# Attention's sums over keys: one 512-column matmul for the high and low parts of the weights in place of two of 256

## The chip, the cores and the metric

The kernel runs on one core of a Trainium2 chip. The metric is the device time of one execution in microseconds; the time before is the median of three runs. The profile is of one more execution, taken by the hardware profiler.

## What is computed

One decoder layer on 2048 tokens of width 1024, float32. Two groups of eight heads (64 wide) attend causally: a stick-breaking group (reference, cut) and a forgetting group; each group's output is normed per head and goes through one output projection, and a gated MLP with a short convolution follows.

```
# stick-breaking, z = q k / 8, strictly causal
log_a = log_sigmoid(z) + (sum over later keys of log_sigmoid(-z))
a     = where(strict, exp(log_a), 0);   out = a @ v
# forgetting, F = cumsum(log f)
p     = softmax(where(causal, q k / 8 + F[t] - F[s], -inf));   out = p @ v
```

The change is in the step `a @ v` or `p @ v`, the sum over keys.

## The kernel before

Each float32 operand of a matmul is split in two: a high part that the matmul's rounded format (fp32r) holds, and a low part, the difference. A product is then summed from high times high, high times low and low times high. `split` (lines 43 to 45) makes the parts: ACT writes the high one, DVE or POOL subtracts it from the source.

Stages, by time in the trace: from 0 to some 90 us the conditioning, the first norm and projection; to some 925 us the stick-breaking group; to some 1610 us the forgetting group; then the output projection, the MLP's up-projection (from 1800 us) and the down-projection (from 2670 us to the end). While attention runs, the projections of later heads (lines 268 and 310) are put between its steps on PE, a few at a time, by `fill_proj`.

Attention works by **units** (a pair of heads and 512 queries; 32 of them), in each four **heads** (`Head`: one head and 256 queries, `j2` and `hl`), in each head some **items** that make the weights for up to 512 keys, and for each pair of key tiles a **group** (`Group`: 2 tiles of 128 keys by 2 tiles of 128 queries). There are 128 heads and 576 groups. 128 of the groups lie on the diagonal (`diag`, one for each head): there the later keys with the earlier queries give nothing, and that quarter is zero.

A stick-breaking item: two matmuls make the logits (lines 368, 369), ACT takes two sigmoids (457, 458), DVE runs a product scan along the keys (463, 466, 470), and POOL multiplies (471), which gives the weights `a`, queries on partitions. A forgetting item: DVE adds the decay and takes the running minimum (510), ACT the exponential (515).

A group then has two steps. `turn` (line 377): PE transposes its four 128 by 128 blocks into one PSUM bank `ps_pt` (383; three where the group is diagonal); on the diagonal POOL writes zeros into the missing quarter of both parts of `at` (386); ACT copies the bank to the high part (387); DVE subtracts to get the low part (388). `at` has three buffers and holds `[2 parts, 4 blocks of 128]` with the blocks in the order (second key tile, query 0), (first, 0), (first, 1), (second, 1). `add` (line 390): four matmuls into the head's PSUM bank `ps_pv`, which has one buffer: for each of the two key tiles, the high and then the low part, 256 queries wide. The stationary operand is V of that key tile and head, 64 columns of its high part beside 64 of its low part, so rows 0 to 63 of the result are V's high part and rows 64 to 127 its low part; all four matmuls add to the same 256 columns. A group's `add` is called two groups after its `turn`.

```
for w in range(2):
    rhs = at[:, w].rearrange("p (s q) -> p s q", q=P)[:, 0:4:3, :] if kk else at[:, w, P:3 * P]
    nc.tensor.matmul(o[:, 0:2 * P], head.V[kt // 4][:, kt % 4, head.hl, :], rhs, ...)
```

`finish` (line 418) ends a head: ACT copies rows 64 to 127 to `o2` (421), DVE adds them to rows 0 to 63 into `oT` (422). After the second of two heads POOL squares `oT` (556, `sq`), PE sums the squares some groups later (561), and after the fourth an SP DMA stores `oT` (426).

The program's order on each engine is set when it is built: the tile framework schedules by an own model of the time, from the order of the code. Each engine runs its queue in order, and waits are on semaphores that the framework places.

Of the kernel before, what the change touches and what calls it, by code (L numbers as in the profile page):

```python
# [8 lines left out]
F32 = mybir.dt.float32  # L9
F32R = mybir.dt.float32r  # L10
BF16 = mybir.dt.bfloat16
AF = mybir.ActivationFunctionType
# [4 lines left out]
P = 128  # L17
# [3 lines left out]
HD = 64  # L21
# [12 lines left out]
def kernel(ctx: ExitStack, tc: tile.TileContext, x, c, w_ada, b_ada, g_attn, w_in, b_fgate,  # L34
                      g_out_fox, g_out_sb, w_out, g_mlp, w_up, conv_w, conv_b, w_down, g_final, out):
    nc = tc.nc
# [3 lines left out]
    def f(t):  # L40
        return t.bitcast(F32)
# [91 lines left out]
    def open_pool(name, side=None, space=None):  # L133
        st = pools[name] = ExitStack()
        kw = dict(space=space) if space is not None else {}
        return st.enter_context(tc.tile_pool(name=name, bufs=1, side=side, reuse_waits="tile", **kw))
# [8 lines left out]
    sb = open_pool("sb", side="right")  # L145
# [226 lines left out]
    class Group:  # L372
# [5 lines left out]
        def turn(self):  # L378
            b = pt()
            self.at = at = sb.tile([P, 2, 2 * 2 * P], F32R, name="at", bufs=3)  # L380
            for i, (kk, qi) in enumerate([(1, 0), (0, 0), (0, 1), (1, 1)]):
                if not (self.diag and i == 0):
                    nc.tensor.transpose(b[:, i * P:(i + 1) * P], self.blk(self.kts[kk], qi), ident)  # L383
            lo = P if self.diag else 0
            if self.diag:
                nc.gpsimd.memset(f(at[:, :, 0:P]), 0.0)
            nc.scalar.activation(at[:, 0, lo:], b[:, lo:], AF.Copy)  # L387
            nc.vector.tensor_sub(at[:, 1, lo:], b[:, lo:], f(at[:, 0, lo:]))  # L388

        def add(self):  # L390
            head, at = self.head, self.at
            if self.first:
                head.o = pv()
            o = head.o
            for kk, kt in enumerate(self.kts):
                for w in range(2):
                    rhs = at[:, w].rearrange("p (s q) -> p s q", q=P)[:, 0:4:3, :] if kk else at[:, w, P:3 * P]
                    nc.tensor.matmul(o[:, 0:2 * P], head.V[kt // 4][:, kt % 4, head.hl, :], rhs,  # L398
                                     start=self.first and kk == 0 and w == 0, stop=self.last and kk == 1 and w == 1)
            if self.last:  # L400
                head.finish()

    class Head:
# [13 lines left out]

        def finish(self):
            o, oT, hl, j2 = self.o, self.unit.oT, self.hl, self.j2
            o2 = sb.tile([HD, 2 * P], F32, name="o2", bufs=2)  # L420
            nc.scalar.activation(o2, o[HD:P, 0:2 * P], AF.Copy)
            nc.vector.tensor_add(oT[hl * HD:(hl + 1) * HD, j2 * 2 * P:(j2 + 1) * 2 * P], o[0:HD, 0:2 * P], o2)
            if hl:
                self.unit.head_var(j2)
                if j2:
                    nc.sync.dma_start(os_[self.unit.mp][self.unit.tb], oT)
# [48 lines left out]
    class FoxItem:  # L475
# [11 lines left out]
        def weights(self, qi, ch):  # L487
            head, n = self.head, self.head.n
            W = (2 * head.j + qi + 1) * P
            Fb = Fbs[head.unit.p][head.hl]  # L490
            ls = head.unit.ls
            if ch == 0:
                self.mn = None
                if n > 2:
                    self.rows[qi] = sx.tile([P, S], F32, name="p", bufs=4)
                elif qi == 0:
                    both = sx.tile([P, S], F32, name="p", bufs=4)
                    self.rows = [both[:, 0:S // 2], both[:, S // 2:S]]
            a = self.rows[qi]
            need = min(512, W - ch * 512)  # L500
            b = logits(max(need, 2 * P), head.qcols(qi), head.hl, head.Q, head.K[ch])
            cuts = [(0, need, Fb[ch][:, :need])]
            if ch == n - 1:
                diag = sx.tile([P, P], F32, name="Fd", bufs=3)
                nc.gpsimd.affine_select(out=diag, in_=Fb[ch][:, need - P:need], pattern=[[-1, P]],
                                        base=0, channel_multiplier=1, compare_op=ALU.is_ge, fill=BIG)
                cuts = [(0, need - P, Fb[ch][:, :need - P])] * (need > P) + [(need - P, need, diag)]
            for lo, hi, add in cuts:
                m2 = sx.tile([P, 1], F32, name="mn", bufs=8)
                nc.vector.tensor_tensor_reduce(out=a[:, ch * 512 + lo:ch * 512 + hi], in0=b[:, lo:hi], in1=add,  # L510
                                               scale=1.0, scalar=3e38 if self.mn is None else self.mn, op0=ALU.add,
                                               op1=ALU.min, accum_out=m2)
                self.mn = m2
            if ch == n - 1:
                nc.scalar.activation(a[:, 0:W], a[:, 0:W], AF.Exp, scale=-1.0, bias=self.mn,
                                     accum_out=ls[:, head.hl, head.qc + qi:head.qc + qi + 1])
# [569 lines left out]
    def load(k, tb):  # L1086
        n = P if k < NFULL else REST
        g = dp.tile([P, 2, TB], F32R, name="g", bufs=6)
        wraw = dp.tile([P, D], F32, name="wdraw", bufs=3)
        graw = dp.tile([P, TB], F32, name="graw", bufs=2)  # L1090
        w = dp.tile([P, 2, D], F32R, name="wd", bufs=6)
        for r in range(P // n):
            nc.sync.dma_start(wraw[r * n:(r + 1) * n], w_down[k * P:k * P + n, :])
            nc.sync.dma_start(graw[r * n:(r + 1) * n], gs[k][tb // 2][:, tb % 2 * TB:(tb % 2 + 1) * TB])
        split(w[:, 0], w[:, 1], wraw, nc.vector)
        if n == P:
            split(g[:, 0], g[:, 1], graw)
        else:
            nc.scalar.activation(g[:, 0], graw, AF.Copy)
            nc.vector.tensor_sub(g[REST:P, 0], graw[REST:P], f(g[REST:P, 0]))  # L1100
        return g, w
# [6 lines left out]
    for tb in range(NTB):  # L1108
# [13 lines left out]
        for k in range(NKD):  # L1122
            g, w = load(k, tb)
# [55 lines left out]
```

## Time and profile before

| | |
|---|---|
| median of 3 runs | 3153.06 us (3152.79 to 3157.4) |
| span of the profiled execution | 3151.1 us |
| PE busy in it | 2971.6 us, 94% |
| PE weight loads | 2517.7 us, 80% |
| DVE, ACT, POOL busy | 68%, 53%, 41% |
| the sums over keys (line 398) | 2304 matmuls, 437.8 us busy |
| granted TensorE clock | 0.98 of full speed over the span |

A matmul's busy time includes the modelled drain of its pipeline; what it keeps from the next matmul is the distance from start to start, which is read from merged rows of the timeline. Idle time stands with the instruction that it precedes, and names what ended it. The chain of waits is followed back from the last instruction.

### The profile page before, as it was taken

What the parts mean: (1) busy time and instruction counts of PE and PEld (TensorE: products, weight loads), DVE (VectorE), ACT (ScalarE), POOL (GpSimd) and SP (SyncE); (2) the same over time, 40 slices, a digit from 0 to 9 for tenths busy, and PEclk for the clock granted to TensorE, in tenths of its full rate; (3) what the DMA queues carried; (4) which work ended last, traced back from release to release, by engine and by line L of the source; (5) the groups of instructions that cost most, each with busy time, mean ns of one, the idle gap of its engine ahead of it and who ended that gap; (6) DMA issues with size and microseconds to landing.
All of it is one profiled execution on the core that took longest, in us unless ns stands there. A gap on an engine that the chain in (4) does not pass through costs nothing.

```text
span 3151.1 us, 46387 instructions
## 1 busy us (share of the span) xinstructions
PE 2971.6 (94%) x15934; PEld 2517.7 (80%) x15934; DVE 2138.4 (68%) x3422; ACT 1655.3 (53%) x3033; POOL 1306.8 (41%) x1459
## 2 busy tenths in 40 slices
PE   7889898989989999999999999999899998999998
PEld 5778797878878889887877778888678887888887
DVE  6776689787976776556743577777987776254253
ACT  5565577666765565556743444444544444343332
POOL 2673566666653242242212244444444442332321
PEclk8999999999999999999999999999999999999999
DMA  9439633654236685685546632222222223554552
GB/s 266 169 133 300 193 106 97 215 180 134 76 115 213 219 288 180 185 301 169 170 153 219 213 96 85 83 88 85 84 81 82 87 86 123 190 201 158 192 200 90
DMA packets 292939, 496.51 MB, mean 158 GB/s; under 512 B 29448, under 2 KB 177664, under 8 KB 291680
## 3 DMA queue, kind: packets, MB, share of 16 engines
q1 hardware_dynamic: 281072, 480.92, 47.9%
q10 hardware_dynamic: 11632, 12.63, 1.1%
q8 instruction: 126, 2.06, 0.3%
q14 instruction: 109, 0.89, 0.1%
HBM read 352.61 MB, written 90.51 MB: 141 GB/s over the span
## 4 chain that ended last, share of the span: by engine, by line
PE 51%; DVE 14%; DMA 13%; POOL 9%; issue 7%; ACT 4%; SPq 2%; POOLq 0%; DVEq 0%; ACTq 0%
PE ps_pj L268 8%; PE ps_o L1118 8%; PE ps_pv L398 6%; PE ps_pt L383 5%; PE ps_pj L310 5%; PE ps_o L968 4%; PE ps_t L1118 4%; PE ps_bc L1118 4%; DMA wuraw<-in_w_up_dram 3%; PE ps_qk L368 3%; DVE wu L45 3%; PE ps_qk L369 3%; DMA hp<-hs 2%; DVE u L1037 2%; POOL ws L956 2%
## 5 line engine op out<-in xcount | busy, mean ns | idle before, releaser
L968 PE MATMUL ps_o<-oa,wu 128*128 128x512 f32 x2088 | 502.7, 392 | 12.6 <-DVE oa L45 5.8
L968 PEld LDWEIGHTS ps_o<-oa,wu 128*128 128x128 f32 x2088 | 391.1, 188 | 102.5 <-DVE oa L45 9.6
L398 PE MATMUL ps_pv<-at,V 128*128 128x256 f32 x2304 | 437.8, 300 | 21.3 <-DVE at L388 8.8
L388 DVE TENSOR_TENSOR at<-ps_pt,at 128x512 fp32r<-128x512 f32 (+1 forms) x576 | 365.1, 650 | 122.4 <-ACT at L387 119.6
L268 PE MATMUL ps_pj<-hp,w_qk 128*128 128x512 f32 x1512 | 417.2, 407 | 17.7 <-DMA hp<-hs 5.5
L387 ACT ACTIVATE at<-ps_pt 128x512 fp32r<-128x512 f32 (+1 forms) x576 | 319.1, 576 | 193.0 <-PE ps_pt L383 132.5
L471 POOL TENSOR_TENSOR a<-a,rw 128x512 f32<-128x512 f32 (+2 forms) x272 | 317.2, 1176 | 234.8 <-DVE rw L466 68.3
L398 PEld LDWEIGHTS ps_pv<-at,V 128*128 128x128 f32 x2304 | 341.8, 192 | 57.9 <-DVE at L388 18.5
L268 PEld LDWEIGHTS ps_pj<-hp,w_qk 128*128 128x128 f32 x1512 | 276.2, 192 | 73.6 <-DMA hp<-hs 7.2
L45 DVE TENSOR_TENSOR wd<-wdraw,wd 128x1024 fp32r<-128x1024 f32 x88 | 112.7, 1280 | 261.9 <-ACT wd L44 261.8
L45 POOL TENSOR_TENSOR g<-graw,g 128x512 fp32r<-128x512 f32 x84 | 142.7, 1702 | 325.8 <-ACT g L44 325.8
L368 PE MATMUL ps_qk<-K,Q 128*128 128x512 f32 (+2 forms) x640 | 260.7, 408 | 14.9 <-ACT a L458 7.1
L466 DVE TENSOR_TENSOR_SCAN rw<-rw 128x512 f32<-128x512 f32 x168 | 251.4, 1509 | 18.0 <-ACT rw L457 16.9
L1118 PE MATMUL ps_o<-wd,g 128*128 128x512 f32 x1040 | 251.1, 391 | 8.7 <-ACT g L44 8.7
L968 PE MATMUL ps_t<-ob,wu 128*128 128x512 f32 x984 | 244.0, 393 | 0.0
L310 PE MATMUL ps_pj<-w_v,hp 128*128 128x256 f32 (+1 forms) x1536 | 230.8, 293 | 9.8 <-DVE V L45 4.6
L369 PE MATMUL ps_qk<-K,Q 128*128 128x512 f32 (+2 forms) x640 | 236.7, 371 | 0.0
L1118 PEld LDWEIGHTS ps_o<-wd,g 128*128 128x128 f32 x1040 | 196.2, 189 | 49.9 <-ACT g L44 9.1
L44 ACT ACTIVATE wu<-wuraw 128x512 fp32r<-128x512 f32 x214 | 133.2, 626 | 195.8 <-PE ps_o L968 132.4
L383 PE MATMUL ps_pt<-edge,a 128*128 128x128 f32 x1088 | 189.8, 280 | 43.0 <-POOL a L471 37.5
L310 PEld LDWEIGHTS ps_pj<-w_v,hp 128*128 128x128 f32 x1536 | 209.8, 195 | 17.3 <-issue 8.7
L968 PEld LDWEIGHTS ps_t<-ob,wu 128*128 128x128 f32 x984 | 187.0, 190 | 39.4 <-ACT hf_m L873 0.2
(222 smaller groups left out, 5753.7 us busy)
## 6 DMA issues: line engine op xcount, KB each, us to landing
hp<-hs SPq DMA_DIRECT2D x224, 512.0 KB
wuraw<-in_w_up_dram SPq DMA_DIRECT2D x84, 512.0 KB
wdraw<-in_w_down_dram SPq DMA_DIRECT2D x84, 512.0 KB
Q<-q SPq DMA_DIRECT2D x128, 256.0 KB
g<-u SPq DMA_DIRECT2D x42, 512.0 KB
graw<-g SPq DMA_DIRECT2D x84, 256.0 KB
hs<-hp SPq DMA_DIRECT2D x32, 512.0 KB
K<-q SPq DMA_DIRECT2D x128, 128.0 KB
```

What stands on the lines that cost most here:

```text
L45: (lo_engine or nc.gpsimd).tensor_sub(lo, src, f(hi))
L268: nc.tensor.matmul(acc, w[kt][:, a, n], h[:, bb], start=kt == 0 and i == 0, stop=kt == KT - 1 and i == 2)
L310: nc.tensor.matmul(av[:, t * width:(t + 1) * width], hts[kt][:, a, tok], w[1][kt][:, bb, 0:width], start=kt == 0 and m == 0, stop=kt == KT ...
L368: nc.tensor.matmul(b[:, :cw], Q[:, hl, 0, qcols], K[:, hl, :cw], start=True, stop=False)
L369: nc.tensor.matmul(b[:, :cw], Q[:, hl, 1, qcols], K[:, hl, :cw], start=False, stop=True)
L383: nc.tensor.transpose(b[:, i * P:(i + 1) * P], self.blk(self.kts[kk], qi), ident)
L387: nc.scalar.activation(at[:, 0, lo:], b[:, lo:], AF.Copy)
L388: nc.vector.tensor_sub(at[:, 1, lo:], b[:, lo:], f(at[:, 0, lo:]))
L398: nc.tensor.matmul(o[:, 0:2 * P], head.V[kt // 4][:, kt % 4, head.hl, :], rhs, start=self.first and kk == 0 and w == 0, stop=self.last and ...
L471: nc.gpsimd.tensor_mul(a[:, :need], a[:, :need], r[:, 1:need + 1])
L968: nc.tensor.matmul(b, w[:, p, j], o[:, q], start=first and i == 0, stop=last and i == 2, skip_group_check=True)
L1118: nc.tensor.matmul(banks[t][n], g[:, a, t * P:(t + 1) * P], w[:, b, n * TB:(n + 1) * TB], start=k == 0 and i == 0, stop=k == NKD - 1 and i ...
```

## The change

On PE, `add` takes two matmuls for a group instead of four. The moving operand is both parts of two blocks, 512 columns; the high part's sums go to columns 0 to 255 of the bank, the low part's to columns 256 to 511. On the diagonal the second key tile's matmul covers only the later query tile, 2 times 128 columns, so nothing reads the empty quarter and POOL no longer writes zeros. `finish` has three sums to add instead of two: ACT copies two pieces out of PSUM, DVE adds the third from PSUM, and POOL adds the last two into `oT`. V's low part times the weights' low part, which was in the sum before, is left out. `o2` has the same room, but one buffer of all 128 partitions instead of two of 64.

```diff
             lo = P if self.diag else 0
-            if self.diag:
-                nc.gpsimd.memset(f(at[:, :, 0:P]), 0.0)
             nc.scalar.activation(at[:, 0, lo:], b[:, lo:], AF.Copy)
             nc.vector.tensor_sub(at[:, 1, lo:], b[:, lo:], f(at[:, 0, lo:]))
...
             for kk, kt in enumerate(self.kts):
-                for w in range(2):
-                    rhs = at[:, w].rearrange("p (s q) -> p s q", q=P)[:, 0:4:3, :] if kk else at[:, w, P:3 * P]
-                    nc.tensor.matmul(o[:, 0:2 * P], head.V[kt // 4][:, kt % 4, head.hl, :], rhs,
-                                     start=self.first and kk == 0 and w == 0, stop=self.last and kk == 1 and w == 1)
+                if not kk:
+                    out_, rhs = o, at[:, :, P:3 * P]
+                elif self.diag:
+                    out_, rhs = o.rearrange("p (w q) -> p w q", w=2)[:, :, P:2 * P], at[:, :, 3 * P:4 * P]
+                else:
+                    out_, rhs = o, at.rearrange("p w (s q) -> p w s q", q=P)[:, :, 0:4:3, :]
+                nc.tensor.matmul(out_, head.V[kt // 4][:, kt % 4, head.hl, :], rhs,
+                                 start=self.first and kk == 0, stop=self.last and kk == 1)
...
-            o2 = sb.tile([HD, 2 * P], F32, name="o2", bufs=2)
-            nc.scalar.activation(o2, o[HD:P, 0:2 * P], AF.Copy)
-            nc.vector.tensor_add(oT[hl * HD:(hl + 1) * HD, j2 * 2 * P:(j2 + 1) * 2 * P], o[0:HD, 0:2 * P], o2)
+            o2 = sb.tile([P, 2, 2 * P], F32, name="o2", bufs=1)[hl * HD:(hl + 1) * HD]
+            nc.scalar.activation(o2[:, 0], o[HD:P, 0:2 * P], AF.Copy)
+            nc.scalar.activation(o2[:, 1], o[0:HD, 2 * P:4 * P], AF.Copy)
+            nc.vector.tensor_add(o2[:, 0], o[0:HD, 0:2 * P], o2[:, 0])
+            nc.gpsimd.tensor_add(oT[hl * HD:(hl + 1) * HD, j2 * 2 * P:(j2 + 1) * 2 * P], o2[:, 0], o2[:, 1])
```

Lines from the loop on move by 2, those behind `finish` by 4: the sums are line 400 now, the copies 423 and 424, DVE's add 425, POOL's 426, the square 560.

What stands in the queues, on PE in a late unit of the forgetting group, around the end of a pair of heads, before:

```order
L268 MATMUL ps_pj<-hp,w_qk 128x512 x11
L398 MATMUL ps_pv<-at,V 128x256
L268 MATMUL ps_pj<-hp,w_qk 128x512
L368 MATMUL ps_qk<-K,Q 128x512
L369 MATMUL ps_qk<-K,Q 128x512
L268 MATMUL ps_pj<-hp,w_qk 128x512
L398 MATMUL ps_pv<-at,V 128x256 x3
L383 MATMUL ps_pt<-edge,p 128x128 x4
L398 MATMUL ps_pv<-at,V 128x256 x4
```

and with the change:

```order
L268 MATMUL ps_pj<-hp,w_qk 128x512 x2
L368 MATMUL ps_qk<-K,Q 128x512
L369 MATMUL ps_qk<-K,Q 128x512
L400 MATMUL ps_pv<-at,V 128x512 x2
L383 MATMUL ps_pt<-edge,p 128x128 x4
L400 MATMUL ps_pv<-at,V 128x512 x2
```

A group's first matmul stood apart from the other three, ahead of filler; now both stand together, behind the filler. Across attention the filler between the sums is dealt out anew in the same way, here as there.

On POOL at the end of the stick-breaking group, in the heads with the most keys, before:

```order
L471 TENSOR_TENSOR a<-a,rw 128x512 [waits DVE_49,PE_49,Activation_49] x2
L386 MEMSET at 128x2x128 [waits DVE_49,PE_49]
L471 TENSOR_TENSOR a<-a,rw 128x512 [waits DVE_49,Activation_49] x2
L556 TENSOR_TENSOR sq<-oT 128x256 [waits DVE_49]
L471 TENSOR_TENSOR a<-a,rw 128x512 [waits DVE_49,Activation_49] x2
```

and at the end of that group's last heads with the change:

```order
L426 TENSOR_TENSOR oT<-o_9990 64x256 [waits DVE_49,Pool_49]
L560 TENSOR_TENSOR sq<-oT 128x256 [waits Pool_49]
L509 AFFINE_SELECT Fd<-Fb 128x128 [waits DMAHW2_49]
```

The zeroing, which waited for PE to be done with the buffer, is gone; the head's add stands in POOL's queue ahead of the square and waits for DVE (`AFFINE_SELECT`, line 505 before and 509 now, masks the decay for the first forgetting heads).

On ACT, at the end of a forgetting head, before:

```order
L387 ACTIVATE at<-ps_pt 128x384
L421 ACTIVATE o_15689<-ps_pv 64x256
L387 ACTIVATE at<-ps_pt 128x512
L515 ACTIVATE p,ls<-p,mn 128x768
L387 ACTIVATE at<-ps_pt 128x512
```

and with the change:

```order
L385 ACTIVATE at<-ps_pt 128x384
L423 ACTIVATE o_14913<-ps_pv 64x256
L424 ACTIVATE o_14913<-ps_pv 64x256
L385 ACTIVATE at<-ps_pt 128x512
L44 ACTIVATE V<-ps_pj 128x4x64
```

The second copy stands right behind the first, and the framework signals both with one step of the semaphore behind the second, so DVE's add waits for both.

## Rows read from the trace of the kernel before

**Rows 1.** The page: busy time, share of the span and instructions of each engine.

```profile
PE 2971.6 (94%) x15934; PEld 2517.7 (80%) x15934; DVE 2138.4 (68%) x3422; ACT 1655.3 (53%) x3033; POOL 1306.8 (41%) x1459
```

**Rows 2.** Stretches of 100 us: length, busy us and count of each engine, clock, DMA.

```profile
core 0: us, PE busy (x) PEld busy (x) DVE busy (x) ACT busy (x) POOL busy (x), PEclk, DMA share, GB/s
500.00:600.00 100.00, 87.09 (x587) 76.41 (x586) 88.08 (x114) 72.55 (x161) 71.25 (x91) 1.00 0.38 111
800.00:900.00 100.00, 84.01 (x573) 72.94 (x572) 97.50 (x110) 77.46 (x159) 70.00 (x76) 0.97 0.16 49
1300.00:1400.00 100.00, 99.51 (x648) 89.24 (x647) 58.23 (x165) 55.16 (x101) 35.04 (x49) 1.00 0.75 249
1500.00:1600.00 100.00, 96.45 (x629) 82.97 (x628) 80.19 (x230) 67.34 (x111) 17.97 (x39) 1.00 0.46 150
2000.00:2100.00 100.00, 99.80 (x439) 81.87 (x438) 76.54 (x90) 44.81 (x65) 41.93 (x41) 1.00 0.26 79
```

**Rows 3.** The chain of waits through attention, 90 to 1610 us, by line.

```profile
by line: PE ps_pj L268 17.3%; PE ps_pv L398 12.4%; PE ps_pt L383 10.2%; PE ps_pj L310 9.2%; PE ps_qk L368 5.5%; issue 5.3%; PE ps_qk L369 5.1%; DMA hp<-hs 4.6%; DVE rw L466 3.2%; POOL a L471 2.9%; DVE at L388 2.3%; DMA hp<-in_w_ada_dram 2.1
```

**Rows 4.** PE's waits in that stretch: us in total, times, longest us.

```profile
PE ps_pt L383 <- POOL a L471: 37.5, 35, 3.0
PE ps_pv L398 <- DVE at L388: 8.8, 19, 1.2
...
PE ps_pv L398 <- ACT at L387: 6.8, 7, 1.7
...
PE ps_pv L398 <- DVE oT L422: 4.6, 7, 1.1
```

**Rows 5.** PE's timeline near 1325 us: start, us from first start to last end.

```profile
1323.02 1.11 PE L398 MATMUL ps_pv<-at,V 128*128 128x256 f32 x8
1323.98 0.38 PE L383 MATMUL ps_pt<-edge,p 128*128 128x128 f32 x2
1324.11 0.72 PE L398 MATMUL ps_pv<-at,V 128*128 128x256 f32 x4
...
1326.05 0.39 PE L268 MATMUL ps_pj<-hp,w_qk 128*128 128x512 f32 x1
...
1326.74 3.12 PE L268 MATMUL ps_pj<-hp,w_qk 128*128 128x512 f32 x13
```

**Rows 6.** Line 398 alone: count, ns min/median/max; waits of both PE rows.

```profile
L398 PE MATMUL ps_pv<-at,V x2304: 274/282/682, 80.8 to 1611.6; 128*128 128x256 f32 x192
...
  DVE at L388: 27.3, 56
  ACT at L387: 21.7, 28
  DVE oT L422: 10.3, 13
```

**Rows 7.** Groups by line: busy us, mean ns, idle us before and what ended it.

```profile
L398 PE MATMUL ps_pv<-at,V 128*128 128x256 f32 x2304 | 437.8, 300 | 21.3 <-DVE at L388 8.8 <-ACT at L387 7.4 <-DVE oT L422 4.6
...
L421 ACT ACTIVATE o<-ps_pv 64x256 f32<-64x256 f32 x128 | 48.9, 382 | 47.2 <-PE ps_pv L398 44.6
...
L422 DVE TENSOR_TENSOR oT<-ps_pv,o 64x256 f32<-64x256 f32 x128 | 52.7, 412 | 24.8 <-ACT o L421 22.9
...
L386 POOL MEMSET at<- 128x256 f32 x128 | 39.8, 312 | 172.9 <-PE ps_pv L398 150.4 <-PE ps_pt L383 9.8 <-DVE V L45 6.4
...
L556 POOL TENSOR_TENSOR sq<-oT 128x256 f32<-128x256 f32 x64 | 50.9, 795 | 67.2 <-DVE oT L422 65.1 <-PE ps_pj L310 1.0 <-PE ps_pt L561 0.8
```

**Rows 8.** POOL's multiply and square by line: count, ns min/median/max.

```profile
L471 POOL TENSOR_TENSOR a<-a,rw x272: 405/1092/2318, 268.7 to 906.4; 128x512 f32<-128x512 f32 x84, 128x128 f32<-128x128 f32 x26, 128x384 f32<-128x384 f32 x26
...
L556 POOL TENSOR_TENSOR sq<-oT x64: 609/615/1632, 93.5 to 1612.8; 128x256 f32<-128x256 f32 x64
```

**Rows 9.** POOL's timeline in a late stick-breaking unit.

```profile
514.15 2.97 POOL L471 TENSOR_TENSOR a<-a,rw 128x512 f32<-128x512 f32 x2 [0.97 <-DVE rw L466]
517.08 1.52 POOL L556 TENSOR_TENSOR sq<-oT 128x256 f32<-128x256 f32 x1
518.57 3.05 POOL L471 TENSOR_TENSOR a<-a,rw 128x512 f32<-128x512 f32 x2
```

## The prediction

> **What bounds the kernel now.** I read the page's busy shares first: PE is busy 94% of the span, DVE 68%, POOL 41% [rows 1]. An average says little here, so next come stretches of 100 us. In the forgetting half of attention PE is at 99.5 and 96.5 of 100 us, DVE at 58 and 80; in the late stick-breaking units DVE is at 88 and 97.5 while PE is at 87 and 84, and POOL at 70; in the MLP PE is full, and nothing of the change is there [rows 2]. So there are two kinds of stretch in attention: one where PE sets the pace and one where DVE and POOL do. The chain of waits from 90 to 1610 us says how they mix: the six PE lines that it lists come to 17.3 + 12.4 + 10.2 + 9.2 + 5.5 + 5.1 = 59.7% of the 1520 us, the line of the change alone to 12.4% or 188 us; DVE's scan, POOL's multiply and the `at` subtraction come to 8.4% [rows 3]. PE's largest wait is for POOL's multiply, 37.5 us [rows 4].
>
> **PE, full pairs.** A busy PE is not a full PE, so a matmul's price is its distance from start to start. Eight sums in a row take 1.11 us, the last with its own length of 0.28: (1.11 - 0.28) / 7 = 0.119 us for 256 columns [rows 5, 6]. Thirteen matmuls of 512 columns take 3.12 us, the last 0.39: 2.73 / 12 = 0.2275 us [rows 5]. So two of 256 cost 0.238, one of 512 costs 0.2275, and 0.0105 us is saved: halving the count hardly helps, since the columns streamed are the same. Of 576 groups with two key tiles each, 1152 pairs, 128 are the diagonal's second tile; the other 1024 save 10.8 us.
>
> A rule speaks against even that. The Trainium skill, "TensorE: Matmul & The Clock Gate", section "Back-to-back issue gap", puts the distance at the columns over 2.4 GHz and some 2.5 ns more, by which a pair would save only that one 2.5 ns. By an estimate from it the full pairs would give 2.6 us; the rows here have about 12 ns beside the columns at both sizes, and the measurement decides.
>
> **PE, the diagonal.** There the second tile's two matmuls of 256 columns become one of 256 (2 times 128): 128 x 0.119 = 15.2 us. Together 26.0 us of streaming, which is the safe part.
>
> **PE, waits inside a group.** The four sums at 1324.11 take 0.72 us, (0.72 - 0.28) = 0.44 for three steps instead of 0.36: 0.08 us is lost within the group, and the eight at 1323.02 lose nothing [rows 5]. The high-part matmul waits for ACT, the low-part one for DVE; a load of V that stands behind a wait isn't hidden. With one wait and one load fewer in a group this can shrink: by nothing at least, by 576 x 0.08 = 46 us at most. I take a quarter of the groups, 12 us, nearer to the row without loss. The price: the first sum can no longer start on the high part alone, so a wait for DVE (27.3 us in 56 times for both PE rows, [rows 6]) now stands ahead of both sums; since it was waited out within the group before, I put no more on it. So PE gets 38 us back (26 to 72).
>
> **How much of it reaches the end.** By the share of the chain on PE, 0.6: 23 us. From below, by the share of the line's own busy time that is on the chain, 188 of 437.8 us or 0.43 [rows 3, 7], 11 us of the streaming; from above all 72.
>
> **The longer end of a head.** ACT copies a second piece, 0.382 us [rows 7], and DVE's add (0.412 us as before) waits for both. `ps_pv` has one buffer, so the next head's first sum is released 0.382 us later, and on PE everything behind it stands in line. Sums waited for DVE's `oT` 13 times in both PE rows [rows 6], of 128 heads: 13 x 0.382 = 5 us. From below nothing, since the framework deals the filler anew; from above 127 x 0.382 = 48.5 us, if every next sum stood ready. I take 5, as the rows show few waits there. ACT itself does 128 x 0.382 = 49 us more, at 53% of the span busy and 72 to 77 in the busiest stretches [rows 1, 2]. No ACT line is among the first of the chain [rows 3], so between 0 and 49 I take 2.
>
> **POOL.** The zeroing goes: 128 x 0.312 = 39.8 us of work, and 172.9 us of standing in front of it, 150.4 of it until PE was done with `at` [rows 7]. In comes an add of 64 x 256 for each head. The nearest row is the square of 128 x 256: 0.615 us in the middle, 1.632 at most [rows 8], so 128 adds are 79 to 209 us, 39 to 169 more than the zeroing. Each waits for DVE, as the square did (65.1 us before 64 squares, [rows 7]), and behind it in POOL's queue stand the multiplies of the next heads, for which PE waits. So one head-of-line wait replaces another, and I count only the work: in the stick-breaking half 64 heads x (0.615 - 0.312) = 19 us, of which POOL's share where PE waits for it, about a sixth: 3 us. From above 64 x 1.32 = 84 us, from below minus 10 us, since the wait before the zeroing goes. `o2` has one buffer: the next head's first copy waits for this add, and a whole head's work lies between the two, so I cost it at nothing; if POOL is late by more than that, ACT stands still, and with it every `at`. On SP the store of `oT` now waits for POOL instead of DVE, some 0.6 us later, with loads of `hp` behind it; 32 stores, 19 us at most, nothing as long as loads run ahead: nothing.
>
> **Sum.** 23 - 5 - 2 - 3 = 13 us less. Profiled span 3151.1 us, median 3153.06, so 2 us or 0.06% lie around the span; the median becomes 3153.06 - 13 = **3140 us**.
>
> **Rivals.** (a) All of PE's time comes back, with half of the waits inside the groups: 26 + 23 = 49 us, 3104 us. For it: PE above 96% in the forgetting half; against it: DVE at 97.5 of 100 us late in the stick-breaking half [rows 2], where PE's gain is only idle time. (b) PE's gain is hidden: PE waits out what it saved for DVE's scan and POOL's multiply, and costs eat the rest: 3153 us, within 6. It is the case if the filler of projections is used up sooner and the stick-breaking units then run at DVE's pace; for it the 59.7% that leave 40% of the chain elsewhere [rows 3]. (c) Slower, by POOL in the stick-breaking half. The square took 1.52 us between two pairs of multiplies that followed without a gap [rows 9]; an add of that length instead of a zeroing of 0.31 is 1.2 us later for the multiplies behind it. If each of the 35 times that PE waits for a multiply [rows 4] grows by 1.2 us, that is 42 us, against 23 gained and 7 of other costs: 26 us slower, 3179 us. It decides from 16 us on, 0.46 us for each of those waits.
>
> On the length of that add: the multiplies take 1.09 us in the middle and up to 2.3 [rows 8], two lengths for one kind of work. The Trainium skill, "SBUF — State Buffer", section "SBUF: two separate sides", has DVE instructions with two inputs in SBUF and POOL's reads take the same pair of ports in turn, the whole instruction long; by it the add is long where DVE is busiest, which is where (c) needs it. The spread of the multiplies agrees; who held the port no row here shows.
>
> (d) The order. Filler, sums and transposes stand otherwise in every queue, as in the piece of PE's queue shown with the change; that is worth some 15 us either way, an estimate of one PE wait of the size seen (37.5 us in 35 times, about 1 us each, [rows 4]) for about each second of the 32 units.
>
> **Chances.** The sum as forecast, from 3128 to 3147: 0.40; (a) and what lies between it and the forecast: 0.20; (b): 0.20; (c), or (d) to that side: 0.20. A measurement of this kernel can tell some 0.2%, 6 us, from no change. So faster 0.60, same 0.20, slower 0.20. The range of 8 in 10 reaches to (a) halfway and to the middle of (c): 3110 to 3166.
>
> **What would show it.** After: 1152 sums with 0.23 us between starts, weight loads halved, PE's busy time down by about 26 us plus drains; 128 more ACT copies of 0.38 us; no zeroing on POOL. If PE's idle time grows by as much as its streaming falls, (b) holds. If the new add takes over 1 us in the stick-breaking half and PE's wait for the multiply grows beyond 37.5 us, (c) holds. If sums wait for DVE's add in far more than 13 heads, the head's end was underpriced. If starts of 512-column sums lie further apart than 0.2275 us, for instance because the moving operand is now four strips of 128 columns, 10 ns more would take 10 us from the gain and 20 ns all of the full pairs'.

## The result and the profile after

The changed kernel takes **3184.16 us** in the median, the kernel before 3154.23 in the runs beside it: ratio **1.0093, interval 1.0081 to 1.0104**, some 29 us slower where 13 us less were forecast, and above the top of the range (3166). The profiled execution of after took 3191.87 us with a span of 3190.0; the last sum of attention ends at 1645 us instead of 1612, and the up-projection starts at 1837.5 instead of 1798.9, as much later as the span is longer: the loss is made ahead of the MLP, most of it in attention. Within attention most of it falls in the stick-breaking group: ACT's first copy at the end of the 64th head, the last of that group, comes at 945.7 us instead of 918.7, and that of the 128th at 1645.7 instead of 1611.9, so 27 of 34 us are lost by then.

The page's busy times, to be read beside [rows 1]:

```profile
PE 2975.5 (93%) x14782; PEld 2446.4 (77%) x14782; DVE 2157.1 (68%) x3422; ACT 1694.2 (53%) x3161; POOL 1376.1 (43%) x1459
```

The edit is all there: 1152 matmuls fewer on PE, 128 copies more on ACT, POOL with as many instructions as before (an add for each zeroing) and 69 us more work. Yet PE's busy time hasn't fallen (the last section, on the granted clock, has part of the reason). Stretches of after, the last line the sums over five stretches from 90 to 1650 us; columns as in [rows 2]:

```profile
90.00:400.00 310.00, 270.56 (x1465) 224.69 (x1464) 209.04 (x273) 179.32 (x389) 180.97 (x213) 0.92 0.59 189
800.00:900.00 100.00, 88.96 (x497) 72.60 (x496) 94.85 (x108) 73.18 (x156) 68.23 (x74) 0.93 0.25 81
1300.00:1400.00 100.00, 96.41 (x588) 83.67 (x586) 57.44 (x173) 55.72 (x116) 35.68 (x54) 0.98 0.58 182
1500.00:1600.00 100.00, 93.11 (x529) 74.93 (x528) 81.22 (x250) 75.03 (x141) 27.56 (x53) 0.98 0.50 153
...
sum 1560.00, PE 1423.66 PEld 1179.72 DVE 1150.14 ACT 1006.51 POOL 799.92; mean PE 284.73 PEld 235.94 DVE 230.03 ACT 201.30 POOL 159.98
```

The forgetting half, where PE was full (99.5 and 96.5 in [rows 2]), has pauses now: 96.4 and 93.1. In the same 1560 us of before the sum was:

```profile
sum 1560.00, PE 1453.62 PEld 1277.13 DVE 1137.26 ACT 981.07 POOL 730.87; mean PE 290.72 PEld 255.43 DVE 227.45 ACT 196.21 POOL 146.17
```

PE is busy 30 us less in this stretch: the streaming that the edit takes away, and some of the work behind attention that now falls outside. PE got time back and spent it waiting. For what, line 400 alone shows (count, ns min/median/max; then waits of both PE rows, us and times), beside [rows 6]:

```profile
L400 PE MATMUL ps_pv<-at,V x1152: 274/396/799, 84.1 to 1645.3; 128*128 128x512 f32 x192
...
  DVE at L386: 68.4, 78
  DVE o L425: 8.4, 13
```

Waits for ACT's high part (21.7 us) are gone, those for DVE's low part went from 27.3 to 68.4 us. The waits for the head's add are as before, 13 times. The groups by line (busy us, mean ns | idle us before and what ended it), beside [rows 7]:

```profile
L386 DVE TENSOR_TENSOR at<-ps_pt,at 128x512 fp32r<-128x512 f32 (+1 forms) x576 | 364.1, 649 | 112.3 <-ACT at L385 109.5
...
L475 POOL TENSOR_TENSOR a<-a,rw 128x512 f32<-128x512 f32 (+2 forms) x272 | 313.1, 1161 | 197.5 <-DVE rw L470 51.0 <-DVE rw L467 39.5 <-PE ps_pt L383 29.6
...
L426 POOL TENSOR_TENSOR oT<-o 64x256 f32<-64x256 f32 x128 | 124.0, 969 | 189.9 <-DVE o L425 174.6 <-DVE var L571 6.8 <-PE ps_qk L369 3.3
...
L425 DVE TENSOR_TENSOR o<-ps_pv,o 64x256 f32<-64x256 f32 x128 | 52.9, 414 | 37.4 <-ACT o L424 22.1 <-PE ps_pj L268 5.6 <-PE ps_qk L369 2.0
...
L560 POOL TENSOR_TENSOR sq<-oT 128x256 f32<-128x256 f32 x64 | 49.6, 776 | 5.0 <-PE ps_pt L565 2.1
```

POOL's new add stands 189.9 us idle, nearly all for DVE. But the zeroing and the square stood 172.9 + 67.2 us idle before [rows 7]: POOL waits less than it did. The sums of waits alone don't say where 29 us went, so the parts were run one by one.

### The profile page after: what moved, and what is told of

Its sections match the earlier page's. It is cut to its first block, busy times and chain, and to the rows that moved or that the text cites. A ratio compares the mean times of both kernels' runs of the same rounds, so it can differ in the third digit from the quotient of the medians.

```text
span 3190.0 us, 44409 instructions
## 1 busy us (share of the span) xinstructions
PE 2975.5 (93%) x14782; PEld 2446.4 (77%) x14782; DVE 2157.1 (68%) x3422; ACT 1694.2 (53%) x3161; POOL 1376.1 (43%) x1459
## 4 chain that ended last, share of the span: by engine, by line
PE 42%; DVE 13%; DMA 10%; issue 7%; POOL 7%; ACT 3%; SPq 1%; POOLq 0%; ACTq 0%; DVEq 0%
PE ps_o L1122 7%; PE ps_pj L268 6%; PE ps_pv L400 4%; PE ps_t L1122 4%; PE ps_bc L1122 4%; PE ps_pt L383 4%; DMA wuraw<-in_w_up_dram 3%; PE ps_o L972 3%; DVE wu L45 3%; PE ps_pj L310 2%; PE ps_qk L368 2%; PE ps_qk L369 2%; DVE u L1041 2%; DMA hp<-hs 2%; POOL ws L960 2%
## 5 line engine op out<-in xcount | busy, mean ns | idle before, releaser
L400 PE MATMUL ps_pv<-at,V 128*128 128x512 f32 (+1 forms) x1152 | 373.4, 415 | 29.8 <-DVE at L386 26.0
L368 PE MATMUL ps_qk<-K,Q 128*128 128x512 f32 (+2 forms) x640 | 265.1, 415 | 18.9 <-DVE mn L514 11.4
L470 DVE TENSOR_TENSOR_SCAN rw<-rw 128x512 f32<-128x512 f32 x168 | 258.6, 1551 | 23.1 <-ACT rw L461 21.8
L400 PEld LDWEIGHTS ps_pv<-at,V 128*128 128x128 f32 x1152 | 196.0, 195 | 68.6 <-DVE at L386 42.4
L369 PE MATMUL ps_qk<-K,Q 128*128 128x512 f32 (+2 forms) x640 | 240.0, 376 | 0.0
L383 PE MATMUL ps_pt<-edge,a 128*128 128x128 f32 x1088 | 192.4, 285 | 47.0 <-POOL a L475 36.1
L383 PEld LDWEIGHTS ps_pt<-edge,a 128*128 128x128 f32 x1088 | 140.8, 147 | 102.0 <-POOL a L475 55.3
```

Of the source, the lines that this page charges most:

```text
L368: nc.tensor.matmul(b[:, :cw], Q[:, hl, 0, qcols], K[:, hl, :cw], start=True, stop=False)
L369: nc.tensor.matmul(b[:, :cw], Q[:, hl, 1, qcols], K[:, hl, :cw], start=False, stop=True)
L400: nc.tensor.matmul(out_, head.V[kt // 4][:, kt % 4, head.hl, :], rhs, start=self.first and kk == 0, stop=self.last and kk == 1)
```

## The experiments

Differences in us are the ratio's, times 3154; the interval of a ratio stands beside it.

**Which part: the head's end or the sums.** The head's end alone, on the kernel before (ACT copies some values a second time with a scale of 0, POOL adds these zeros):

```diff
+ o2 = sb.tile([P, 2, 2 * P], F32, name="o2", bufs=1)[hl * HD:(hl + 1) * HD]
  nc.scalar.activation(o2[:, 0], o[HD:P, 0:2 * P], AF.Copy)
+ nc.scalar.activation(o2[:, 1], o[0:HD, 0:2 * P], AF.Copy, scale=0.0)
+ nc.vector.tensor_add(o2[:, 0], o[0:HD, 0:2 * P], o2[:, 0])
+ nc.gpsimd.tensor_add(oT[...], o2[:, 0], o2[:, 1])
```

> The kernel before with the change's end of a head alone: its four sums of 256 columns and its zeroing stay; ACT makes a second copy (of sums already there, scaled by zero, so that nothing is added), DVE adds, POOL adds into oT, o2 has one buffer. Theory 1, the longer end of a head is the cause (POOL's add in front of the multiplies, a PSUM bank released later): slower than before by 20 us or more, 3174 to 3200. Theory 2, the merged sums are the cause (both now wait for the low part): 3154 to 3164. Theory 3, any edit deals the queues out anew and that alone moves the time: anywhere from 3140 to 3175, with no growth of the waits for DVE's add or POOL's multiply.

Measured (e1) 3187.24 us, 1.0102 (1.0080 to 1.0124): +32 us, the whole loss. In its profile 31 us are lost by the end of the 64th head (949.9 us) and 32 by that of the 128th (1643.7): all of it in the stick-breaking group.

The sums alone: the changed sums with the head's end of before, so the low parts of the weights are summed but left out of the result.

```diff
- nc.scalar.activation(o2[:, 1], o[0:HD, 2 * P:4 * P], AF.Copy)
- nc.vector.tensor_add(o2[:, 0], o[0:HD, 0:2 * P], o2[:, 0])
- nc.gpsimd.tensor_add(oT[...], o2[:, 0], o2[:, 1])
+ nc.vector.tensor_add(oT[...], o[0:HD, 0:2 * P], o2)
```

> The changed kernel with the end of a head as before (one copy, one add on DVE, no add on POOL, two buffers of o2): the sums of the low part of the weights, columns 256 to 511, are computed and left out of the result. Theory 1 (the end of a head): the gain of the sums is seen, 3130 to 3145. Theory 2 (the merged sums' wait): still slower than before, 3165 to 3185, and PE's waits of sums for DVE stay near 68 us in both PE rows. Theory 3: 3140 to 3175.

Measured (e2) 3152.37 us, 0.9995 (0.9984 to 1.0006): nothing. So there are two questions: why the end costs 32 us, and why 1152 matmuls fewer bring none.

**The end, piece by piece.** Only the second copy, unread, so that ACT works 49 us more and the bank is released 0.38 us later:

```diff
+ nc.scalar.activation(o2[:, 1], o[0:HD, 0:2 * P], AF.Copy)
```

> The kernel before with ACT's second copy alone at the end of a head (the same 64 by 256 piece once more, into a buffer that nobody reads; o2 has one buffer); DVE adds into oT as before, POOL is untouched. The end of a head as a whole cost 32 us. Theory 1a, the copy is the cause (0.38 us more on ACT, and the PSUM bank released 0.38 us later): 3170 to 3187. Theory 1b, POOL's add is the cause: 3150 to 3162.

Measured (e5) 3158.01 us, 1.0004 (0.9994 to 1.0015): ACT's work and the later release cost 0 to 5 us. Only POOL's add, of zeros, with DVE's add writing to `o2`:

```diff
+ nc.vector.tensor_add(o2, o[0:HD, 0:2 * P], o2)
+ nc.gpsimd.tensor_add(oT[...], o2, edge[...])
```

> The kernel before with POOL's add alone: ACT copies once, DVE adds into o2, and POOL adds zeros to that, into oT; the PSUM bank is released as early as before, o2 has two buffers. Theory 1b (oT later, and POOL's queue held by an add that waits for DVE): 3170 to 3187. Theory 1a: 3150 to 3162. If both cost half: 3165 to 3172 for each of the two.

Measured (e6) 3191.30 us, 1.0117 (1.0102 to 1.0132): +37 us. The add is the price. Two runs put it on DVE instead, once from `o2` and once straight from PSUM with one copy less:

```diff
- nc.gpsimd.tensor_add(oT[...], o2[:, 0], o2[:, 1])
+ nc.vector.tensor_add(oT[...], o2[:, 0], o2[:, 1])
```

> The changed kernel with the last add of a head on DVE in place of POOL. If POOL's add is the cause within theory 1: back to 3150 to 3165, and POOL's 175 us of standing before the add are gone. If it is the later release of the PSUM bank or the merged sums: 3175 to 3195, DVE having 0.4 us more for each of 128 heads.

```diff
- nc.scalar.activation(o2[:, 1], o[0:HD, 2 * P:4 * P], AF.Copy)
- nc.gpsimd.tensor_add(oT[...], o2[:, 0], o2[:, 1])
+ nc.vector.tensor_add(oT[...], o[0:HD, 2 * P:4 * P], oT[...])
```

> The changed kernel with one ACT copy and two adds on DVE, the second adding the low part's sums from PSUM into oT: no second copy on ACT and no POOL, but the bank is released 0.41 us later than before, as late as in the changed kernel. If the later release of the bank is the cause: 3170 to 3185, as the changed kernel with its last add on DVE (3176.7). If ACT's extra copy in its queue is the cause: 3150 to 3160.

Measured (e3) 3176.67 us, 1.0072 (1.0051 to 1.0093), and (e7) 3181.80 us, 1.0084 (1.0069 to 1.0099): +23 and +26 us. Elsewhere, then, but not gone. Both lie in the ranges expected for the later release of the bank, but e5 has that at 0 to 5 us, so the numbers alone don't name it.

**Why the add on POOL costs: its work, or what it waits for.** On the kernel before, one POOL add more in each head, into the unread half of `o2`: once of constants, once of `oT` (which DVE wrote as early as before) and constants.

```diff
+ nc.gpsimd.tensor_add(o2_unread_half, zero, zero)      # e9
+ nc.gpsimd.tensor_add(o2_unread_half, oT[...], zero)   # e10
```

> The kernel before, with one more POOL add of 64x256 in each of the 128 heads, zeros plus zeros into the unread half of o2: the work of the new add (0.73 us in the middle in the profile of after, 94 us in all) without any wait for DVE. If POOL's time itself is the price of the add, because the multiplies behind it come that much later: most of the 36 us that POOL's add cost in e6_pool_add_alone, 3180 to 3190. If the price is the waiting in POOL's queue for DVE's add, or the later oT: within 10 us of before, 3150 to 3165.

> The kernel before, DVE writes oT as it did, and one more POOL add in each head reads oT and writes the unread half of o2: the work of the new add and its wait for DVE, but oT is complete as early as before. If work is the price: as e9_pool_work. If the wait at the head of POOL's queue is: 3180 to 3190 here and near before in e9_pool_work. If it is the later oT (square and store wait for it): near before in both, 3150 to 3165.

Measured (e9) 3154.44 us, 1.0001 (0.9989 to 1.0013), and (e10) 3176.03 us, 1.0067 (1.0042 to 1.0091). Groups of POOL, of the first and then of the second:

```profile
L426 POOL TENSOR_TENSOR o<-edge 64x256 f32<-64x256 f32 x128 | 96.2, 752 | 15.9 <-DVE oT L425 5.7
...
L560 POOL TENSOR_TENSOR sq<-oT 128x256 f32<-128x256 f32 x64 | 53.3, 832 | 56.4 <-DVE oT L425 52.6 <-DMA wos<-hp 2.4 <-ACT hp L660 0.3
```

```profile
L426 POOL TENSOR_TENSOR o<-oT,edge 64x256 f32<-64x256 f32 x128 | 115.5, 902 | 144.8 <-DVE oT L425 128.5 <-DVE var L571 3.5 <-ACT w_v L44 3.4
...
L560 POOL TENSOR_TENSOR sq<-oT 128x256 f32<-128x256 f32 x64 | 50.5, 789 | 7.4 <-PE ps_pt L565 2.5
```

96 us of work that waits for nothing cost nothing; 115 us of work that waits for DVE cost 21 us. The wait ahead of the square went into the add, and 80 us came on top (144.8 + 7.4 against 15.9 + 56.4 us idle). Between this run (+21) and the add alone (+37) the intervals do not touch: that `oT` itself comes through POOL, and later, costs some 16 us more; this part was seen only as that difference.

The two runs differ in more than the wait. With nothing to wait for, 127 of e9's 128 adds start ahead of ACT's copy at the end of their head, 12 us ahead in the middle; e10's all start behind it, 1.8 us in the middle. So the work is free where it can run early, and costs where it is bound to the head's end; the wait and the place in the queue are not separated here.

**Fewer waits in line.** If a step that waits at the head's end is the price, taking some away must give it back. The squares on ACT, in the kernel before and in the changed kernel:

```diff
- nc.gpsimd.tensor_mul(sq, self.oT[:, cols_], self.oT[:, cols_])
+ nc.scalar.activation(sq, self.oT[:, cols_], AF.Square)
```

> The kernel before, with the 64 squares of 128x256 on ACT instead of POOL: 39 us of work (0.61 us each) and 65 us of waiting for DVE leave POOL's queue, some 25 us of work come to ACT, whose time was free in e5_copy_alone. If POOL's work or its waiting in line sets the pace in the stick-breaking half: faster by 5 to 20 us, 3135 to 3150. If only the later oT costs: within 6 us of before.

> The changed kernel with the squares on ACT, the adds of each head still on POOL. If waiting at the front of POOL's queue is the price: about 12 us less than the changed kernel, as in e11_square_on_act, near 3170, since the 128 waits of the adds stay. If the later oT is the price, because the square on POOL comes late: back to before, 3150 to 3160, as in e12_pair_add.

Measured (e11) 3142.73 us, 0.9960 (0.9945 to 0.9975), and (e13) 3176.03 us, 1.0064 (1.0046 to 1.0082): 13 us less than before, and 9 less than the changed kernel's 1.0093, whose interval touches. **The first beats both kernels.** The add once for two heads, with the squares on POOL, and with the squares on ACT:

```diff
+ if hl:
+     nc.gpsimd.tensor_add(oT[:, both heads], o2_pair[:, 0], o2_pair[:, 1])
```

> The changed kernel with POOL's add once for two heads, 128x256 instead of twice 64x256, the squares still on POOL right behind it. 64 waits for DVE in POOL's queue in place of 128 and the square no earlier than before. If waiting in line is the price: 12 to 20 us less than the changed kernel, 3164 to 3172. If the later oT and square are: no better than the changed kernel, 3178 to 3190.

> The changed kernel with POOL's add once for two heads, 128x256 instead of twice 64x256, and the squares on ACT. POOL then does 64 adds in place of before's 64 squares and 64 zeroings. If POOL's work or its waiting is what the change lost by: the 29 us come back, 3145 to 3160, and below before if the sums' 26 us of streaming then reach the end. If the later oT is the price: 3170 to 3185 still, since the square comes later than ever.

Measured (e14) 3171.83 us, 1.0049 (1.0032 to 1.0066), and (e12) 3158.52 us, 1.0015 (1.0004 to 1.0026): 14 and 25 of the 29 us come back. POOL's group of the first of the two:

```profile
L430 POOL TENSOR_TENSOR oT<-o 128x256 f32<-128x256 f32 x64 | 55.7, 870 | 121.6 <-DVE o L428 114.4 <-PE ps_qk L369 5.4 <-PE ps_pt L383 1.8
```

Half as many adds, each for 128 partitions, make half the work (55.7 for 124.0 us), and the wait falls to 121.6 from 189.9. The later `oT` as the only price falls here: the square stands as late as in the changed kernel, and time comes back all the same. That the zeroing's wait is of the same kind, the last run on POOL's queue was to tell: e11 with the zeroing on ACT as well.

```diff
- nc.gpsimd.memset(f(at[:, :, 0:P]), 0.0)
+ nc.scalar.activation(at[:, :, 0:P], zeros, AF.Copy)
```

> The kernel e11_square_on_act with the 128 zeroings of the diagonal's quarter on ACT as well: 39 us of work and 127 us of waiting for PE leave POOL's queue, some 50 us of work come to ACT. If any wait at the front of POOL's queue has a price: 5 to 12 us below e11, 3130 to 3138. If only waits for DVE in the stick-breaking half do, or ACT's time now counts: 3140 to 3155.

Measured (e16) 3162.40 us, 1.0024 (1.0012 to 1.0036): 20 us worse than e11, and above both ranges expected. ACT's 128 zeroings, 0.411 us in the middle, stand right ahead of ACT's own copy of the same `at`; 49 us of copies at the head's end were free (e5), 53 us there are not. Whether POOL's queue gained anything by it can't be read from this run.

**The price of DVE's time.** The kernel before with an add of constants on DVE in each head:

```diff
+ nc.vector.tensor_add(o2_unread_half, zero, zero)
```

> The kernel before, with one more DVE add of 64x256 in each head, zeros plus zeros into the unread half of o2: DVE's time alone, some 0.4 us each and 50 us in all, with no wait of its own. If DVE sets the pace in the stick-breaking half: that half's share of it, 15 to 30 us slower, and with it the 22 us of e3_add_on_dve are explained by work. If DVE has room: within 6 us of before, and the add on DVE cost by its waiting too.

Measured (e15) 3192.68 us, 1.0120 (1.0100 to 1.0141): +38 us. Its group on DVE:

```profile
L426 DVE TENSOR_TENSOR o<-edge 64x256 f32<-64x256 f32 x128 | 75.1, 587 | 4.0
```

75 us of DVE work, waiting for nothing, cost half of themselves, although these adds too start ahead of the head's end. DVE is 68% busy and POOL 41% [rows 1]; work that can run early is free on POOL and dear on DVE. With it the 23 and 26 us of the add on DVE (e3, e7) need no other cause than the work.

**Why the sums bring nothing.** Two runs on the sums of before, the same four matmuls of 256 columns: high parts of both key tiles first, then the low ones; and in each tile the low part first.

```diff
- for kk, kt in enumerate(self.kts):
-     for w in range(2):
+ for w in range(2):                    # e8
+     for kk, kt in enumerate(self.kts):
```

> The kernel before with its four sums in another order: both key tiles' high parts first, then both low parts; the same work on every engine, the zeroing and the end of a head as before. Theory 3, the dealing of the queues alone moves the time: beyond 10 us either way. Theories 1a and 1b: within 8 us of before, 3147 to 3163; a little faster if it helps that two sums can start on the high part alone.

```diff
-     for w in range(2):
+     for w in (1, 0):                  # e18
```

> The kernel before with the two matmuls of each key tile in the order low part, high part: the same four matmuls of 256 columns and the same head's end, but a group of sums starts when DVE has the low part, as in the changed kernel, and not when ACT has the high part. If that later start eats the 26 us of streaming in e2_sums_alone: 10 to 28 us slower than before, 3164 to 3182. If the later start costs nothing and PE's streaming is simply not on the path: within 6 us of before, as e8_order_alone.

Measured (e8) 3156.07 us, 0.9999 (0.9988 to 1.0010), and (e18) 3169.97 us, 1.0055 (1.0038 to 1.0072). This other order by itself is worth nothing, and with it this re-dealing of the queues; but a group whose first matmul waits for the low part costs 17 us. Line 398 of that second run, waits of both PE rows:

```profile
L398 PE MATMUL ps_pv<-at,V x2304: 274/282/563, 83.8 to 1629.1; 128*128 128x256 f32 x192
...
  DVE at L388: 49.1, 55
  DVE oT L422: 11.4, 16
```

and line 400 of the sums alone (e2):

```profile
L400 PE MATMUL ps_pv<-at,V x1152: 274/396/795, 83.4 to 1608.5; 128*128 128x512 f32 x192
...
  DVE at L386: 58.4, 75
  DVE oT L424: 11.7, 16
```

In [rows 6] the group waited 27.3 us for DVE and 21.7 for ACT, 49.0 in all; here 49.1 for DVE alone. The same sum, and 17 us more. My reading of it: in before, the high part's matmul had been done when PE waited within a group, and the changed sums have no such start. The runs show the waits and the price, but not this link itself.

Two more runs on the share of PE's time. The changed kernel with the diagonal's quarter zeroed and summed as before:

```diff
+ nc.gpsimd.memset(f(at[:, :, 0:P]), 0.0)
- elif self.diag:
-     out_, rhs = o[..., P:2 * P], at[:, :, 3 * P:4 * P]
```

> The changed kernel with the diagonal's empty quarter kept: zeroed by POOL and summed, so all 1152 sums have 512 columns. PE streams 128 x 0.108 = 14 us more and POOL does 40 us more. If PE's streaming is worth its share of 0.6: 8 us slower than the changed kernel, 3192. If the cause of the loss lies elsewhere and PE's time does not count: 3180 to 3188.

Measured (e4) 3187.22 us, 1.0102 (1.0087 to 1.0118): 3 us more than the changed kernel, within both intervals; the 15 us of streaming for the quarter and the zeroing together are worth between nothing and some 12 us here. And the sums alone with the squares on ACT (low parts left out again):

> The changed sums with the head's end of before, as e2_sums_alone (the low parts of the weights are summed but left out of the result), and the squares on ACT as in e11_square_on_act. If PE's streaming is not on the path because DVE sets the pace and the sums now wait for DVE: as e11, 3138 to 3148. If it was held back by POOL's queue alone: 10 to 20 us below e11, 3122 to 3133.

Measured (e17) 3151.88 us, 0.9994 (0.9983 to 1.0006): with POOL relieved the new sums are not faster than e11 but 11 us slower. They are no gain waiting to be uncovered. Why they cost 11 us beside squares on ACT and nothing beside squares on POOL, no run shows.

## Why the prediction was wrong, point by point

In the prediction's own terms, the sums were to give 23 us and gave 2 (e2), and the longer end of a head was to cost 5 + 2 + 3 = 10 us and cost 32 (e1). -2 + 32 = 30, and 29 was measured.

- **PE, full pairs, 10.8 us: right.** After a sum whose moving operand lies in two pieces of 256 columns (551 starts of after with the next sum right behind), a quarter of the next ones start within 0.231 us, a twentieth within 0.227; after one of four strips (74) the middle is 0.2315. The forecast's 0.2275 holds for a sum that nothing holds up, and the four strips that it feared cost some 4 ns. The Trainium skill, "TensorE: Matmul & The Clock Gate", section "Back-to-back issue gap", has 512 columns over 2.4 GHz and some 2.5 ns, 215.8 ns by an estimate, which it calls the gap of an isolated matmul; the rows are 11 ns above it.
- **The diagonal, 15.2 us:** as said; its 256-column sums lie 0.117 us apart. As time it was too small to be measured (e4).
- **Waits inside a group: 12 us forecast, 8 found.** What the starts of sums in a row lose against the undisturbed 0.119 and 0.2275 us is 42.0 us in before (349 stalls) and 34.0 in after (298): half of the groups still lose 0.09 us between their two matmuls, 0.318 us instead of 0.23.
- **The start of a group, taken at nothing: the first step that failed.** "Since it was waited out within the group before, I put no more on it." It had been waited out with the high part's matmul already behind it. To start on the low part costs 17 us with the sums of before (e18). With the share of 0.6 the 26 + 8 us would be 20, and 20 - 17 = 3; the sums alone gave 2 (e2, from 5 less to 2 more). So the share may stand; e4, the only run that bears on it by itself, allows anything from 0 to 0.8.
- **The later release, 5 us, and ACT, 2 us:** right in size; together 0 to 5 (e5). The waits for the head's add, 13 times before and after, were the right row to price this by.
- **POOL, 3 us: the second step that failed, and the one that set the sign.** "One head-of-line wait replaces another, and I count only the work." By the sums it is even true, 195 us idle before add and square for 240 before zeroing and square. But the work costs nothing where it can run early (e9), and what costs is the add at the head's end, behind DVE (e10, e14), and that `oT` comes through it. Nor does the stick-breaking half alone tell it: until 985 us zeroing and square had waited 34.8 + 13.9 us in 15 times, the add 54.1 us in 16. Idle time in front of an instruction doesn't say what its lateness costs behind it: of the add's 189.9 us, 136.5 lie in the forgetting half, where 7 of the 34 us were lost. At the end of the 64th head, the kernels with the add are late (after 946 us, e1 and e6 950), and the five runs that cost nothing (e2, e5, e8, e9, e17) stand at 915 to 929.
- **Rival (c), 3179 us, had the engine, the sign, the place and nearly the size, and one of its two marks came.** It wanted the add over 1 us in the stick-breaking half and PE's wait for the multiply above 37.5 us. PE's waits in after, and the add in its first 950 us (ns min/median/max; then busy us, mean ns and idle us, there and from 950 to 1650 us):

```profile
PE ps_pt L383 <- POOL a L475: 36.1, 40, 1.9
PE ps_pv L400 <- DVE at L386: 26.0, 27, 2.8
```

```profile
L426 POOL TENSOR_TENSOR oT<-o x64: 718/776/3177, 91.3 to 947.1; 64x256 f32<-64x256 f32 x64
...
L426 POOL TENSOR_TENSOR oT<-o 64x256 f32<-64x256 f32 x64 | 76.6, 1197 | 53.4 <-DVE o L425 49.1 <-PE ps_pt L383 2.2
...
L426 POOL TENSOR_TENSOR oT<-o 64x256 f32<-64x256 f32 x64 | 47.4, 741 | 136.5 <-DVE o L425 125.5 <-DVE var L571 6.8 <-PE ps_qk L369 3.3
```

  The length came: 1.20 us in the mean, though 0.78 in the middle. PE's wait for the multiply did not grow: 36.1 us, in 40 times instead of 35. So the path on which (c) worked out its 42 us is not what these rows show, and that its number came near is luck; which instruction behind the add carries the delay to the end is not shown by any of these runs.

  One path that the prediction left out is DVE's scans, which in the stick-breaking half run beside POOL's adds. Line 466 before and the same line, 470, after:

```profile
L466 DVE TENSOR_TENSOR_SCAN rw<-rw 128x512 f32<-128x512 f32 x168 | 251.4, 1509 | 18.0 <-ACT rw L457 16.9
```

```profile
L470 DVE TENSOR_TENSOR_SCAN rw<-rw 128x512 f32<-128x512 f32 x168 | 258.6, 1551 | 23.1 <-ACT rw L461 21.8
```

  All 320 scans along the keys took 423.8 us before and 441.7 after. In the seven profiles with a POOL add for each head they took 435 to 449 us, in the thirteen others 407 to 430. At the half that DVE's time cost in e15, 18 us more are 9 of the 29, by an estimate; e9's 11 us more cost nothing that could be measured. The Trainium skill, "SBUF — State Buffer", section "SBUF: two separate sides", lets DVE and POOL lock each other out of a pair of ports. The trace agrees as far as lengths go, with 1.41 us for an add beside a scan and 0.73 for the others (last section); who held a port no row shows.
- **Rival (b), 3153 us,** is what the sums alone came to (3152, e2), and its mark came in after: PE's idle time, the span less its busy time, grew by 35 us where 26 us of streaming fell away. Its reason, the waiting for DVE's scan and POOL's multiply, did not show as such: the sums wait for the low part instead (68.4 us for 27.3). And it too took the head's end far too small.
- **Rival (d), another order, 15 us either way:** e8 put one other order at nothing.
- **The chances:** 0.20 for slower was too little. Two of the costs were of a kind with no row in the trace of before, a dependent step in POOL's queue and a start that waits for the later of two, and both were taken near their lower bounds. The low end of the range, 3110, was also not halfway to (a) as the text has it: from 3140 that is 3122.

## What to carry to other kernels

Price a step added to a chain by what it waits for and what waits behind it, not by its work: 96 us of work on POOL that could run early were free, the same add in the chain cost 37. Where two producers deliver halves at different times, merging their consumers makes both wait for the later one; compare that with the streaming saved before anything else. And an engine's busy share doesn't rank it: 75 us more on DVE at 68% cost 38 us, 49 us more on ACT at 53% nothing, and 53 us on ACT ahead of the copy that DVE and PE wait for 20 us.

## What the runs showed of the hardware

TensorE's granted clock went down with the pauses. From 90 to 400 us it was 0.96 in the mean before and 0.92 after, and from 800 to 900 us 0.97 and 0.93, means between the two levels of 1.2 and 2.4 GHz; PE was busy 280.1 of the first 310 us before and 270.6 after. Taken over 32 stretches of 50 us from 50 to 1650 us, what is missing to the full clock comes to 38.5 us before and 61.5 after. In the nine profiles with the new sums it is 47.0 to 61.5, in the eleven with the old ones 28.5 to 50.5: the two overlap, but fewer matmuls on a path with waits went with a lower clock. At the lower level PE was busy for 109 us of the whole execution before and 148 after; matmuls of 512 columns in a row lie 0.427 us apart there and 0.227 at the upper one, so by an estimate the 39 us more hold some 18 us that the upper level would have saved. That would be much of why PE's busy time did not fall. The clock alone does not set the time: the kernel before, e2, e5, e8, e9 and e17 lie within 0.1% of each other with 28.5 to 47.5 us missing. How much of the 29 us it is, and whether it is cause or effect, no run here separates.

An add's length depends on what it reads, and more on what DVE does beside it. The same 64x256 add on POOL took 0.609 us in the middle on constants (e9) and 0.735 where it read `oT` (e10); on DVE the one on constants ran from 0.418 to 1.495 us, with a mean of 0.587. In the stick-breaking half of after, 44 of the 64 adds on POOL ran beside one of DVE's scans and took 1.41 us in the mean; the 20 others took 0.73, none over 0.74. In e9 it was 1.06 us for 41 beside a scan, and 0.61 for the 23 others; as e9 cost nothing, this length by itself is not the price.
